# A Strassen MLP on one core: seven left operands made one by one, or six of them in pairs

## The chip, the cores and the metric

One core of a Trainium2 chip runs the whole program. A NeuronCore has TensorE (PE: matmuls, with its weight loads listed as PEld), VectorE (DVE), ScalarE (ACT), GpSimd (POOL) and SyncE (SP), which here issues the transfers. Each engine takes the instructions of its own queue in order, and one that needs a result of another engine waits at the head of its queue. The metric is the device time of one launch in microseconds; three launches were timed, and the median counts.

## What is computed

The reference is one step of a two-layer trunk for 1152 tokens (128 context, 1024 latent) of width 1024. Each layer has a mixer, and then the MLP with which this change has to do:

```python
D_MODEL = 1024
DEPTH = 2
D_FF = 4 * D_MODEL
EPS = 1e-6

def rms_norm(x, g):
    xf = x.astype(F32)
    y = xf * lax.rsqrt(jnp.mean(xf * xf, axis=-1, keepdims=True) + EPS)
    return (y * g.astype(F32)).astype(x.dtype)
...
    h2 = rms_norm(x, p['norm2']) * (1 + sc2) + sh2
    x = x + g2 * (jnp.square(jax.nn.relu(h2 @ p['w1'])) @ p['w2'])
```

`sh2`, `sc2` and `g2` come from the conditioning vector. A final RMS norm follows the last layer. Everything is float32. The kernel gets near that by splitting each operand of a product into a high part in the matmul's format and a low part, which is the remainder, and by adding three products of parts: high·high, high·low and low·high.

## The kernel before

**Seven products instead of eight.** Both products of the MLP are tiled in blocks of two by two, and each block product is formed with seven products of sums of blocks (the Strassen-Winograd form). For one block of `w2` (a *version* of the left operands, four quarters `a11`, `a12`, `a22`, `a21` of 128x256 each), the seven left operands are, in the order of the products 0 to 6: `a11`, `s1 = a22 + a21`, `s2 = s1 - a11`, `a12`, `s3 = a11 - a21`, `s4 = a12 - s2`, `a22`. The right operands come from `hidden_operands`: `B11`, `T1`, `T2`, `B21`, `T3`, `B22`, `T4`, made of the MLP's hidden values, which are read back from `hd` in tiles `xb`.

**The left operands.** `Weights.version` is a generator. For each of the seven it takes one tile `wt` of 128x512, writes the high part with a ScalarE cast (`acopy`, L184) and the low part as a difference (`psub` on POOL, L187, or `vsub` on DVE, L190):

```python
def part(t):
    o = new().rearrange("p (j c) -> p j c", j=2)
    acopy(o[:, 0], t)
    next(subs)(o[:, 1], t, o[:, 0])
    return o
```

`lo_subs(n)` hands n of the seven differences to DVE: four (operands 1, 3, 5, 6) in the first three versions of a layer, two (3, 6) in all others. The raw quarters lie in two tiles `wr` (`a11|a12` and `a22|a21`), the sums `s1` to `s4` in two tiles `wl`, made by four DVE additions of 128x256 per version. The ring `W2_RING` has 11 tiles: `release(i)`, called behind the last use of operand i, makes the operand 10 places after the oldest one not yet released.

**The lines.** `second(g, m, q)` with `Line.products` runs the seven products of one block product. A product is two blocks deep, with three matmuls in each (L1103 high·high, L1104 high·low, L1105 low·high), so 6 matmuls, and 42 in a line:

```python
a = pb("bA")[:, :BLK]
run(a, 0, True)
acopy(bb, a)
...
run(bb, 2)
acopy(bc, bb)
```

Product 0 lies in PSUM tile `bA`; ScalarE copies it to `bB`, product 2 is added there, ScalarE copies that to `bC`; products 3, 4, 5 and 6 are then added to `bA`, `bB`, `bC` and once more `bB`. Product 1 has a tile `bE` of its own. As each sum is complete, an operation `row<-bA`, `row<-bB` or `row<-bC` (DVE in all but the first group: L196, in the last group L208) adds it to the result rows. `Line.add` weaves the first four products of one line between the last ones of the line before; there are two `bB` and two `bC`, used in turn, so product 2 of a line has to wait until the line before the last has left its `bB`.

**Order.** A layer has 64 lines, in 8 groups of the hidden width, and 36 versions (five in the first group, four in each of the six middle ones, seven in the last, where most versions serve one line). The program is written in the order of the calls; a scheduler, which weighs priorities (`tc.high_priority`) and its own estimate of the durations, writes each engine's queue from it. In the last group the norm of the result starts (`rms_rest`), behind which come the next layer's operands or the output `y`.

Of the kernel before, what the change touches and what calls it, by code (L numbers as in the profile page):

```python
# [6 lines left out]
F32 = mybir.dt.float32  # L7
# [36 lines left out]
HALF, BLK, GRID, CTXH = T // 2, T // 4, TS // 2, TP // 2  # L44
W1_RING, W2_RING = (7, 7), 11
MID = (28, 28, 30, 31, 32, 33, 34, 35, 36, 37)
HEAD, FOOT, TAIL = 4, 2, 300
LOADS = 5, 2
URGE1, URGE2 = 400, 400
MLP_MODS = (6, 32)  # L50
W1_SUBS, W2_SUBS = (2, 8, 2, 5), (4, 3, 2)
HIDDEN_SUBS = (0, 0, 1, 0, 0, 1, 1)
# [68 lines left out]
def build(ctx, tc, I, O):  # L121
# [39 lines left out]
    def phase(st, tag, bufs, w=NW, side="left"):  # L161

        pool = st.enter_context(tc.tile_pool(name=tag, bufs=bufs, side=side, reuse_waits="tile"))
        return lambda name, dt=F32: pool.tile([P, w], dt, tag=tag, name=name)
# [48 lines left out]
    def dma(out, in_):  # L213
        return nc.sync.dma_start(out=out, in_=in_)
# [131 lines left out]
    def rms_rest(sq, ps=None, w=P):  # L346
        return rms_turn(rms_scale(sq, ps or pb, w), ps or pb, w)
# [661 lines left out]
    class Ends:  # L1009


        def __init__(self, p5, c11, c12, c21, c22):
            self.p5, self.c11, self.c12, self.c21, self.c22 = p5, c11, c12, c21, c22

    def lo_subs(n):

        return iter([vsub if (i + 1) * n // 7 > i * n // 7 else psub for i in range(7)])

    class Weights:
# [51 lines left out]
        def release(self, i):  # L1071
            self.free.add(i)
            while self.low in self.free:
                self.low += 1
            self.get(min(self.low + self.ring, self.total) - 1)

    class Line:
# [236 lines left out]
    for l in range(DEPTH):  # L1314
# [418 lines left out]
        tp = [two_phases(st0, "tp0", 6, 1, T)]  # L1733
        ring2 = phase(st0, "wt", W2_RING, 4 * P, "right")
        z_ = phase(st0, "z5", 4, BLK, "right")
        tp += [two_phases(st1, "tp1", 5, 2, T), phase(st1, "tp2", 7, T, "right")]

        def group_operands(s):
# [9 lines left out]
            [(m, (0,)) for m in range(KD // 2 - 1)] + [(KD // 2 - 1, (0, 1))] + [(m, (1,)) for m in reversed(range(KD // 2 - 1))]]  # L1748
        weights = Weights([I["w2"][l, g, m] for g in range(NG) for m, _ in order[g]], 2, lambda: ring2("wt", F32R), W2_RING,
                          lambda i: lo_subs(W2_SUBS[0] if i < W2_SUBS[1] else W2_SUBS[2]))  # L1750
        line = Line(banks, weights)

# [69 lines left out]
        for k in range(2):  # L1822
            sums[done[1]].add(rows[2 * done[0] + k])
        rs = [rms_rest(t, pa, (b - a) // 3) for t, (a, b) in zip(sums[1].sq, cut[n0:])]
        if last:
# [131 lines left out]
```

## Time and profile before

| | before |
|---|---|
| three timed runs | 3304.11, 3305.46, 3312.4 us; median 3305.46 |
| profiled execution | 3315.0 us (span 3313.2 us, mean granted clock 0.952) |
| busy, share of the span | PE 90%, PEld 85%, DVE 73%, ACT 50%, POOL 44% |
| second product of the MLP, layer 0 | about 1256 to 1699 us of the span |
| second product of the MLP, layer 1 | about 2841 to 3290 us of the span |

The profiled execution is one of its own, 9.5 us above the median of the three others. A span counts from the first to the last instruction. The shares are means over the whole program; the second product is 443 us of each layer, and what goes on there is read from its own windows. Matmuls overlap in the records, so a busy share near 100% is no proof of the full rate; the number of matmuls in a window says more.

### The profile page before, as it was taken

Reading aid. Unit: us, or ns where it says so; the run is one execution under the profiler, and the core shown is the slowest. Engines: PE = TensorE matmul, PEld = TensorE weight load, DVE = VectorE, ACT = ScalarE, POOL = GpSimd, SP = SyncE. Lnnn points to the kernel's source line nnn. Section 1 sums busy time; section 2 is a strip of 40 time slices with the busy share of each in tenths; the row PEclk is TensorE's granted clock in tenths of the full one; section 3 lists DMA queues with packets and bytes.
Section 4 is the critical chain, followed back from the end, with each engine's and each line's share of the span. In section 5 each row is a group of like instructions: output and inputs, shape, how many; then the busy total and the mean of one; then the engine's idle time right before and its main releaser. Section 6 shows DMA issues by size and latency. Waiting matters only on the chain. (4 is left out here: it accounts for less than half of the span.)

```text
span 3313.2 us, 60910 instructions
## 1 busy us (share of the span) xinstructions
PE 2981.6 (90%) x21208; PEld 2819.6 (85%) x21208; DVE 2415.0 (73%) x5467; ACT 1662.5 (50%) x4089; POOL 1468.4 (44%) x1400
## 2 busy tenths in 40 slices
PE   7888998998888898999868999999989999899985
PEld 6877888798888897899868889988879999789985
DVE  7899973677899967888983677345777223788897
ACT  5543244564644456455454533455637556654443
POOL 4442132444533335666535321334555343565663
PEclk8999999999999998999979999999999999999997
DMA  7342448983455553322422112689534333323242
GB/s 265 92 108 94 131 124 237 279 265 106 137 181 173 171 158 100 96 88 88 128 98 75 58 37 72 192 252 293 184 129 133 106 98 112 111 90 98 93 128 67
DMA packets 363220, 451.11 MB, mean 136 GB/s; under 512 B 64416, under 2 KB 238624, under 8 KB 362912
## 3 DMA queue, kind: packets, MB, share of 16 engines
q1 hardware_dynamic: 362912, 447.22, 44.4%
q8 instruction: 167, 2.74, 0.3%
q14 instruction: 141, 1.16, 0.1%
HBM read 338.29 MB, written 108.79 MB: 135 GB/s over the span
## 5 line engine op out<-in xcount | busy, mean ns | idle before, releaser
L187 POOL TENSOR_TENSOR wl<-wr,wh 128x512 fp32r<-128x512 f32 x164 | 229.4, 1402 | 482.2 <-ACT wh L184 367.8
L187 POOL TENSOR_TENSOR ws<-wl,ws 128x512 fp32r<-128x512 f32 x160 | 222.9, 1397 | 334.9 <-ACT ws L184 327.4
L1103 PE MATMUL bB<-T,wt 128*128 128x288 f32 x768 | 243.0, 318 | 81.5 <-ACT bB L184 46.3
L187 POOL TENSOR_TENSOR wt<-wl,wt 128x256 fp32r<-128x256 f32 x276 | 256.6, 938 | 106.4 <-ACT wt L184 77.0
L1103 PE MATMUL bB<-t,ws 128*128 128x288 f32 x768 | 235.1, 307 | 48.3 <-DVE hr L196 34.8
L211 ACT ACTIVATE hr<-hr 128x288 f32<-128x288 f32 x384 | 170.2, 445 | 200.9 <-DVE hr L196 194.3
L414 PE MATMUL pj<-hh,wh 128*128 128x384 f32 x640 | 223.7, 354 | 24.5 <-ACT g L211 11.4
L280 DVE CUSTOM_DVE_ANT_0 junk<-wm,sil,ma 128x384 bf16<-128x384 f32 (+1 forms) x320 | 233.1, 728 | 10.1 <-DMA wm<-in_w_mod 4.2
L1103 PEld LDWEIGHTS bB<-T,wt 128*128 128x128 f32 x768 | 149.5, 195 | 103.0 <-ACT bB L184 58.0
L1104 PE MATMUL bB<-T,wt 128*128 128x288 f32 x768 | 232.9, 304 | 0.0
L1105 PE MATMUL bB<-T,wt 128*128 128x288 f32 x768 | 231.7, 303 | 0.0
L1105 PE MATMUL bB<-t,ws 128*128 128x288 f32 x768 | 230.0, 300 | 0.0
L1104 PE MATMUL bB<-t,ws 128*128 128x288 f32 x768 | 229.9, 299 | 0.0
L416 PE MATMUL pj<-hh,wl 128*128 128x384 f32 x640 | 225.5, 353 | 4.6 <-POOL wl L187 4.6
L415 PE MATMUL pj<-hh,wh 128*128 128x384 f32 x640 | 224.2, 351 | 0.0
L1103 PEld LDWEIGHTS bB<-t,ws 128*128 128x128 f32 x768 | 147.9, 193 | 60.0 <-DVE hr L196 40.6
L190 DVE TENSOR_TENSOR xb<-xb 128x576 f32<-128x576 f32 (+1 forms) x160 | 169.5, 1061 | 10.0 <-POOL B L187 6.9
L414 PE MATMUL wo<-u,wh 128*128 128x288 f32 x512 | 161.3, 316 | 16.7 <-DVE x L208 13.4
L184 ACT CAST wh<-wr 128x512 fp32r<-128x512 f32 x164 | 101.6, 621 | 129.9 <-PE pj L415 72.4
L1103 PE MATMUL bA<-B,wt 128*128 128x288 f32 x512 | 158.1, 311 | 8.6 <-DVE row L208 3.0
L184 ACT CAST wt<-wl 128x256 fp32r<-128x256 f32 x288 | 115.9, 407 | 91.4 <-PE bB L1105 42.3
L1105 PE MATMUL bA<-B,wt 128*128 128x288 f32 x512 | 156.4, 306 | 3.8 <-POOL wt L187 3.8
(345 smaller groups left out, 11143.0 us busy)
## 6 DMA issues: line engine op xcount, KB each, us to landing
wr<-in_w SPq DMA_DIRECT2D x304, 256.0 KB, 3.0
xb<-hd SPq DMA_DIRECT2D x64, 576.0 KB, 4.0
wm<-in_w_mod SPq DMA_DIRECT2D x160, 192.0 KB, 2.9
wr<-in_w_in SPq DMA_DIRECT2D x104, 256.0 KB, 2.9
bi<-in_bias SPq DMA_DIRECT2D x96, 192.0 KB, 4.4
QS<-qd SPq DMA_DIRECT2D x72, 256.0 KB, 4.3
hd<-hr SPq DMA_DIRECT2D x128, 144.0 KB, 2.8
hd<-hr SPq DMA_DIRECT2D x128, 112.0 KB, 2.1
```

What stands on the lines that cost most here:

```text
L184: nc.scalar.copy(out=out, in_=in_)
L187: nc.gpsimd.tensor_tensor(out=out, in0=a, in1=b, op=ALU.subtract)
L190: nc.vector.tensor_tensor(out=out, in0=a, in1=b, op=ALU.subtract)
L211: nc.scalar.activation(out=out, in_=in_, func=f, **kw)
L280: nc.vector.tensor_tensor_reduce(out=junk[:, :w], in0=r[:, :w], in1=sil[:, c, k0:k0 + w], scale=1.0, scalar=acc[c], op0=ALU.mult, op1=ALU. ...
L414: mm(ps, lhsT=wh(k), rhs=ah(k), start=k == first, stop=False)
L415: mm(ps, lhsT=wh(k), rhs=al(k), start=False, stop=False)
L416: mm(ps, lhsT=wl(k), rhs=ah(k), start=False, stop=k == last)
L1103: mm(ps, lhsT=w[:, 0, ti(i)], rhs=t[:, 0], start=start and i == 0, stop=False, skip_group_check=True)
L1104: mm(ps, lhsT=w[:, 0, ti(i)], rhs=t[:, 1], start=False, stop=False, skip_group_check=True)
L1105: mm(ps, lhsT=w[:, 1, ti(i)], rhs=t[:, 0], start=False, stop=i == n - 1, skip_group_check=True)
```

## The change

Six of the seven left operands are made in three pairs: `a11` with `a12` (products 0 and 3), `s1` with `s3` (1 and 4), `s2` with `s4` (2 and 5). The raw tile `a11|a12` is a pair as it is loaded; the sums are laid into two tiles so that the other pairs stand side by side. One cast and one difference of 128x512 make both high parts and both low parts of a pair; `a22` (product 6) stays alone. The ring of 11 tiles of 128x512 becomes five tiles of 128x1024 (`wt`) and one of 128x512 (`wu`, for `a22`), the same number of bytes. A pair's tile is free when both products have been released, and `wu` when product 6 of the version before has been. The differences' engines are now given for the three pairs and the single: DVE, POOL, DVE, POOL in the first three versions, POOL, POOL, DVE, POOL in the others. The last `rms_rest` is put at a higher priority.

```diff
-W1_RING, W2_RING = (7, 7), 11
+W1_RING, W2_RING = (7, 7), (5, 1)
-URGE1, URGE2 = 400, 400
+URGE1, URGE2, URGE3 = 400, 400, 60
-W1_SUBS, W2_SUBS = (2, 8, 2, 5), (4, 3, 2)
+W1_SUBS = (2, 8, 2, 5)
...
+    def w2_subs(i):
+
+        return (vsub, psub, vsub, psub) if i < 3 else (psub, psub, vsub, psub)
+
...
+    class PairWeights(Weights):
...
+            def part(t, o):
+                acopy(o[:, 0], t)
+                next(subs)(o[:, 1], t, o[:, 0])
+                return o
+
+            def pair(t):
+                o = part(t, new().rearrange("p (j c) -> p j c", j=2))
+                later.append(o[:, :, w:])
+                return o[:, :, :w]
+
+            yield pair(raw[0])
+            s, r = (W.tile([P, DM // 2], F32, tag="wl", name="wl") for _ in range(2))
+            s1, s3, s2, s4 = s[:, :w], s[:, w:], r[:, :w], r[:, w:]
+            vtt(s1, a22, a21, ALU.add)
+            vsub(s3, a11, a21)
+            yield pair(s)
+            vsub(s2, s1, a11)
+            vsub(s4, a12, s2)
+            yield pair(r)
+            yield from later
+            yield part(a22, self.new1().rearrange("p (j c) -> p j c", j=2))
+
+        def ready(self, i):
+
+            v, p = divmod(i, 7)
+            if p == 6:
+                j = v - self.ring[1]
+                return j < 0 or 7 * j + 6 in self.free
+            j, k = divmod(3 * v + p - self.ring[0], 3)
+            return p > 2 or j < 0 or {7 * j + k, 7 * j + k + 3} <= self.free
+
+        def release(self, i):
+            self.free.add(i)
+            while len(self.tiles) < self.total and self.ready(len(self.tiles)):
+                self.get(len(self.tiles))
...
-        ring2 = phase(st0, "wt", W2_RING, 4 * P, "right")
+        ring2, ring1 = phase(st0, "wt", W2_RING[0], 8 * P, "right"), phase(st0, "wu", W2_RING[1], 4 * P, "right")
...
-        weights = Weights([I["w2"][l, g, m] for g in range(NG) for m, _ in order[g]], 2, lambda: ring2("wt", F32R), W2_RING,
-                          lambda i: lo_subs(W2_SUBS[0] if i < W2_SUBS[1] else W2_SUBS[2]))
+        weights = PairWeights([I["w2"][l, g, m] for g in range(NG) for m, _ in order[g]], 2, lambda: ring2("wt", F32R),
+                              lambda: ring1("wu", F32R), W2_RING, lambda i: iter(w2_subs(i)))
...
-        rs = [rms_rest(t, pa, (b - a) // 3) for t, (a, b) in zip(sums[1].sq, cut[n0:])]
+        with tc.high_priority(URGE3):
+            rs = [rms_rest(t, pa, (b - a) // 3) for t, (a, b) in zip(sums[1].sq, cut[n0:])]
```

In the changed kernel the three matmuls stand at L1161, L1162 and L1163. The queues of the two kernels differ within the two second products only; the numbers behind the names count tiles and differ from kernel to kernel.

ScalarE's queue, middle groups of layer 0. Before, the casts of one version are the seven rows `wt` (`wr_18162` is its `a11|a12`, `wr_18164` its `a22|a21`, the `wl` its sums), with the copies of the lines between them:

```order
L184 CAST wt_18166<-wr_18162 128x256
L184 CAST wt_18215<-wl_18213 128x256
L184 CAST wt_18234<-wl_18213 128x256
L184 CAST wt_18251<-wr_18162 128x256
L184 CAST wt_18271<-wl_18269 128x256
L184 COPY bB_10171<-bA_18199 128x288
L184 CAST wt_18290<-wl_18269 128x256
L184 COPY bB_10172<-bA_18262 128x288
L184 CAST B11_18469<-xb_18465 128x576
L184 CAST wt_18307<-wr_18164 128x256
```

ScalarE's queue at a like place in the changed kernel:

```order
L184 CAST wt_17855<-wl_17789 128x512
L184 COPY bB_10171<-bA_17859 128x288
L184 CAST wt_17909<-wr_17905 128x512
L184 CAST T4_18009<-xb_17985 128x576
L184 CAST wt_17916<-wl_17912 128x512
L184 COPY bC_10173<-bB_10171 128x288
L184 CAST wu_17902<-wr_17783 128x256
L184 COPY bB_10172<-bA_17927 128x288
```

Three wide casts and one narrow one now stand for the seven, and the `a22` of a version (`wu_17902`) stands behind the first two pairs of the next one.

POOL's queue at such a place, before (`T3`, `B11`, `T1` and `B21` are low parts of right operands):

```order
L187 TENSOR_TENSOR wt_17920<-wl_17918,wt_17920 128x256
L187 TENSOR_TENSOR T3_17895<-xb_17875,T3_17895 128x576
L187 TENSOR_TENSOR wt_17939<-wl_17918,wt_17939 128x256
L187 TENSOR_TENSOR wt_17976<-wl_17974,wt_17976 128x256
L187 TENSOR_TENSOR B11_18174<-xb_18170,B11_18174 128x576
L187 TENSOR_TENSOR wt_17995<-wl_17974,wt_17995 128x256
L187 TENSOR_TENSOR T1_18178<-xb_18170,T1_18178 128x576
L187 TENSOR_TENSOR wt_18033<-wr_18029,wt_18033 128x256
```

and in the changed kernel:

```order
L187 TENSOR_TENSOR wt_17785<-wr_17781,wt_17785 128x512
L187 TENSOR_TENSOR wt_17792<-wl_17788,wt_17792 128x512
L187 TENSOR_TENSOR wu_17778<-wr_17630,wu_17778 128x256
L187 TENSOR_TENSOR T1_17991<-xb_17983,T1_17991 128x576
L187 TENSOR_TENSOR B21_17999<-xb_17985,B21_17999 128x576
L187 TENSOR_TENSOR T3_18003<-xb_17983,T3_18003 128x576
L187 TENSOR_TENSOR wt_17909<-wr_17905,wt_17909 128x512
L187 TENSOR_TENSOR wt_17916<-wl_17912,wt_17916 128x512
```

A version's low parts on POOL now stand together, and up to three right operands' parts of 128x576 stand between one version's and the next one's.

TensorE's queue in the middle groups of layer 0, around a product 2, before:

```order
L1103 MATMUL bB_10171<-T2_17593,wt_17939 128x288
L1104 MATMUL bB_10171<-T2_17593,wt_17939 128x288
L1105 MATMUL bB_10171<-T2_17593,wt_17939 128x288
L1103 MATMUL bB_10171<-T2_17593,wt_17939 128x288
L1104 MATMUL bB_10171<-T2_17593,wt_17939 128x288
L1105 MATMUL bB_10171<-T2_17593,wt_17939 128x288
```

and in the changed kernel, where `wt_17855` is a pair `s2|s4` and `wt_17785` the pair `a11|a12`:

```order
L1161 MATMUL bB_10171<-T2_17442,wt_17855 128x288
L1162 MATMUL bB_10171<-T2_17442,wt_17855 128x288
L1161 MATMUL bA_17859<-B21_17445,wt_17785 128x288
L1162 MATMUL bA_17859<-B21_17445,wt_17785 128x288
L1163 MATMUL bA_17859<-B21_17445,wt_17785 128x288
L1161 MATMUL bA_17859<-B21_17445,wt_17785 128x288
L1162 MATMUL bA_17859<-B21_17445,wt_17785 128x288
L1163 MATMUL bA_17859<-B21_17445,wt_17785 128x288
L1163 MATMUL bB_10171<-T2_17442,wt_17855 128x288
L1161 MATMUL bB_10171<-T2_17442,wt_17855 128x288
```

Product 2 begins with the two matmuls that need only the high part of `s2`, product 3 stands in between, and the first matmul with the low part (L1163) follows it.

## Rows read from the trace of the kernel before

**Rows 1.** The page's first line and its busy times by engine.
```profile
span 3313.2 us, 60910 instructions
...
PE 2981.6 (90%) x21208; PEld 2819.6 (85%) x21208; DVE 2415.0 (73%) x5467; ACT 1662.5 (50%) x4089; POOL 1468.4 (44%) x1400
```

**Rows 2.** Busy time by window; columns as the first line says.
```profile
core 0: us, PE busy (x) PEld busy (x) DVE busy (x) ACT busy (x) POOL busy (x), PEclk, DMA share, GB/s
1256.00:1350.00 94.00, 77.93 (x474) 73.77 (x475) 79.15 (x102) 59.51 (x154) 63.20 (x54) 0.83 0.31 97
1350.00:1600.00 250.00, 236.30 (x1711) 229.66 (x1711) 212.89 (x397) 124.00 (x293) 151.99 (x142) 0.99 0.31 95
1600.00:1699.00 99.00, 78.32 (x519) 74.23 (x517) 93.97 (x192) 48.19 (x117) 48.21 (x46) 0.89 0.41 128
2740.00:2800.00 60.00, 60.00 (x455) 60.00 (x454) 18.22 (x29) 36.25 (x81) 19.75 (x16) 1.00 0.33 104
2835.00:2950.00 115.00, 95.49 (x625) 90.90 (x625) 91.76 (x127) 69.39 (x178) 70.33 (x62) 0.90 0.32 100
2950.00:3200.00 250.00, 235.07 (x1706) 227.74 (x1705) 216.63 (x400) 123.79 (x293) 152.39 (x142) 1.00 0.33 100
3200.00:3290.00 90.00, 66.55 (x422) 63.16 (x420) 82.08 (x174) 42.98 (x111) 43.67 (x43) 0.84 0.25 77
```

**Rows 3.** TensorE's waits from 1350 to 1600 us: total us, times, longest.
```profile
PE bB L1103 <- ACT bB L184: 9.2, 12, 1.1
PE bB L1103 <- ACT bC L184: 3.4, 4, 0.9
PE bB L1103 <- DVE row L196: 0.7, 3, 0.3
PE bA L1103 <- DVE row L196: 0.3, 1, 0.3
```

**Rows 4.** TensorE's waits from 2950 to 3200 us.
```profile
PE bB L1103 <- ACT bB L184: 9.5, 14, 1.1
PE bB L1103 <- ACT bC L184: 3.9, 5, 0.9
```

**Rows 5.** Timeline of DVE: start, us, instruction, [idle before <- releaser].
```profile
1437.01 1.66 DVE L190 TENSOR_TENSOR wl<-wl,wr 128x256 f32<-128x256 f32 x1
...
1443.05 0.96 DVE L190 TENSOR_TENSOR B<-xb,B 128x576 fp32r<-128x576 f32 x1 [0.23 <-ACT B L184]
1443.93 0.45 DVE L196 TENSOR_TENSOR row<-bB,row 128x288 f32<-128x288 f32 x1
```

**Rows 6.** Timeline of ACT, the same place.
```profile
1444.41 0.38 ACT L184 COPY bB<-bA 128x288 f32<-128x288 f32 x1 [0.47 <-DVE row L196]
```

**Rows 7.** Timeline of PE, the same place.
```profile
1444.85 0.40 PE L1103 MATMUL bB<-T,wt 128*128 128x288 f32 x1 [0.89 <-ACT bB L184]
```

**Rows 8.** Groups by line and shape: busy us, mean ns, idle before and releasers.
```profile
L187 POOL TENSOR_TENSOR wt<-wl,wt 128x256 fp32r<-128x256 f32 x276 | 256.6, 938 | 106.4 <-ACT wt L184 77.0 <-DVE row L196 17.4 <-issue 8.0
L187 POOL TENSOR_TENSOR ws<-wl,ws 128x512 fp32r<-128x512 f32 x160 | 222.9, 1397 | 334.9 <-ACT ws L184 327.4 <-DVE mod L280 4.9 <-DMA hd<-hr 1.9
L184 ACT CAST wt<-wl 128x256 fp32r<-128x256 f32 x288 | 115.9, 407 | 91.4 <-PE bB L1105 42.3 <-PE bA L1105 23.1 <-DVE wl L190 13.8
L184 ACT CAST ws<-wl 128x512 fp32r<-128x512 f32 x160 | 98.3, 618 | 64.4 <-PE bB L1105 23.3 <-PE bC L1105 14.6 <-PE bA L1105 11.9
L190 DVE TENSOR_TENSOR wt<-wr,wt 128x256 fp32r<-128x256 f32 x144 | 94.9, 659 | 19.7 <-ACT wt L184 19.2
L184 ACT CAST wt<-wr 128x256 fp32r<-128x256 f32 x216 | 87.4, 407 | 27.9 <-PE bC L1105 13.2 <-PE bB L1105 6.4 <-PE bA L1105 5.3
L187 POOL TENSOR_TENSOR wt<-wr,wt 128x256 fp32r<-128x256 f32 x72 | 65.1, 904 | 81.1 <-PE bA L1105 38.6 <-ACT wt L184 25.4 <-DVE wl L190 15.5
L190 DVE TENSOR_TENSOR ws<-wr,ws 128x512 fp32r<-128x512 f32 x52 | 41.7, 802 | 18.2 <-ACT ws L184 18.1
```

**Rows 9.** DVE's differences of line 190: duration ns min/median/max, first and last start.
```profile
L190 DVE TENSOR_TENSOR wt<-wr,wt x144: 406/426/1628, 1257.5 to 3262.0; 128x256 fp32r<-128x256 f32 x144
...
L190 DVE TENSOR_TENSOR ws<-wr,ws x52: 676/688/1780, 826.5 to 2829.9; 128x512 fp32r<-128x512 f32 x52
```

**Rows 10.** Timeline of PE at the end of either layer: first matmul of the last product.
```profile
1694.84 0.61 PE L1103 MATMUL bB<-T,wt 128*128 128x288 f32 x1 [9.78 <-DVE row L208]
...
3283.77 0.61 PE L1103 MATMUL bB<-T,wt 128*128 128x288 f32 x1 [7.35 <-DVE row L208]
```

**Rows 11.** Timeline of POOL around the first row of Rows 5.
```profile
1436.50 1.89 POOL L187 TENSOR_TENSOR T<-xb,T 128x576 fp32r<-128x576 f32 x1 [1.40 <-ACT T L184]
```

**Rows 12.** POOL's differences of line 187, 1350 to 1600 us: ns min/median/max.
```profile
L187 POOL TENSOR_TENSOR T<-xb,T x20: 1425/1870/1953, 1366.5 to 1589.6; 128x576 fp32r<-128x576 f32 x20
```

More of the change, by code (lines that the diff above doesn't have):

```diff
@@ L1075, in release, with __init__, version @@
             self.get(min(self.low + self.ring, self.total) - 1)
+    class PairWeights(Weights):
+        def __init__(self, srcs, n, new, new1, rings, subs):
+            self.new1 = new1
+            super().__init__(srcs, n, new, rings, subs)
+        def version(self, src, n, new, subs, spare):
+            w = n * P
+            raw = []
+            for i in range(2):
+                t = W.tile([P, DM // 2], F32, tag="wh" if i else "wr", name="wr")
+                dma(t, src[:, 2 * i * w:2 * (i + 1) * w])
+                raw.append(t)
+            a11, a12 = (raw[0][:, j * w:(j + 1) * w] for j in range(2))
+            a22, a21 = (raw[1][:, j * w:(j + 1) * w] for j in range(2))
+            later = []
+            def part(t, o):
[28 more added lines that the diff above has]
+                self.get(len(self.tiles))
     class Line:
```

## The prediction, made before the changed kernel ran

> **What bounds the kernel now.** I read the page first. TensorE is busy for 90% of the span and ScalarE and POOL, which the change relieves most, for half of it or less [rows 1], so the number to find is not how much work goes away but how much of TensorE's lost time hangs on it. For that the windows over the two second products count matmuls. [...]
>
> Then who is waited for. In the middle, TensorE names almost one thing: product 2 waits for the copy from `bA` to `bB`, 9.2 us in 12 waits and 9.5 in 14; the copy from `bB` to `bC` costs 3.4 in 4 and 3.9 in 5 [rows 3, 4]. [...] No left operand is waited for. The timeline of one such wait gives the chain: DVE's difference for a right operand runs 0.96 us, behind it DVE reads the old `bB` into the rows (0.45), then ScalarE copies (0.38), then the matmul starts after 0.89 us idle [rows 5, 6, 7]. So the wait is the bank's, and the late one is DVE, which is 85% and 87% busy there; in the two last stretches it is busy for 94 of 99 and 82 of 90 us [rows 2], and there it is the bound.
>
> **The change part by part.** Prices first; a 512-wide difference or cast exists already in the first product (`ws`), the same shape and format, so I take its mean.
> DVE: of the 72 versions, 6 (three a layer) lose four differences of 0.659 and get two of 0.802, 1.03 us less each; the other 66 lose two and get one, 0.52 less each [rows 8]. That is 40 us of DVE in all. The wide difference could cost from 0.676, the least seen of its shape, to 1.32, twice the narrow one's mean [rows 8, 9], so 0.52 lies between 0.64 and nothing.
> ScalarE: 504 casts of 0.407 (203 us) become 216 of 0.618 and 72 of 0.407 (163), 40 us less. POOL: 256.6 + 65.1 us become 138 differences of 1.397 and 72 of 0.904 (258), 64 less [rows 8]. Neither is a bound (ScalarE 50%, POOL 61% busy in the middle [rows 2]), so I count these at nothing by themselves; DVE's and TensorE's waits cover them.
> The rest of the instructions, transfers among them, keep their number: raw tiles are loaded as before, and the four sums stay four. The higher priority of the last norm I cost at nothing: without it every queue of the changed kernel comes out in the same order.
>
> What moves is the order. I counted matmuls in TensorE's two queues. From the end of product 6 on a `bB` to the next product 2 on it there were 22 in the mean and now are 26: 4 x 0.132 = 0.53 us more room for the chain above. From the end of product 2 to product 4 on the same bank, which needs the copy to `bC` in between, there were 18 and now are 13: 0.66 us less. And a weight tile's old contents used to be done with 100 matmuls (13 us, median) before the new low part was wanted; in the middle groups it is now 37 (4.9 us), at least 27 (3.6 us), and for a high part 25 (3.3 us), at least 19 (2.5).
>
> A, the middle (1711 and 1706 matmuls of 84 a version make 41 versions [rows 2]): the 26 waits for `bB` average 18.7 / 26 = 0.72 us, so 0.53 more room removes most of each but not all: 26 x 0.53 = 13.8, of which I take 12, since the longest go to 1.1. The 9 waits for `bC` would grow by 0.66 each if each stayed where it is: 9 x 0.66 = 6 lost. What then remains, 6.7 for `bB` and 13.3 for `bC`, 20 us, is still behind DVE's queue, and DVE does 41 x 0.52 = 21 us less. A wait is shortened only where the saved piece stood in front of a read of its bank; no row gives that share, so it lies between 0 and 20, and I take 8, somewhat under half. Sum: -12 + 6 - 8 = -14, with bounds of +6 (no gain on `bB`) and -26 (all 26.0 us of waits gone).
> B, the last groups: DVE is the bound, so its saving counts whole: 7 versions x 0.52 = 3.6 a layer, -7. Against it `wu` is a ring of one tile: the very last `a22` can be cast only when the product 6 before is over, and its chain of 0.407 and 0.904 [rows 8] stands 1 to 3 matmuls ahead of its use. But the last product waits 9.78 and 7.35 us for DVE's rows anyway [rows 10]; I count +1 a layer. Sum: -5.
> C, the starts: three versions x 1.03 = 3.1 a layer on DVE, which is 80 to 84% busy; half of it counts: -3.
> Together -22. The profiled execution took 3315.0 us, of which 3313.2 are the span [rows 1]; it would be 3293. It lies 9.5 over the median of the three runs, which I carry over: 3293 - 9.5 = 3283.5.
>
> [...] First the row: a DVE sum of 128x256 at 1437.01 took 1.66 us [rows 5], where DVE's difference of the same size has a median of 0.426 and a maximum of 1.628 [rows 9]; POOL's difference of 128x576 ran from 1436.50 to 1438.39 [rows 11], and DVE's instruction ended just after it. [...]
>
> **The rivals.**
> Slower: the ring is too short. A pair's tile needs both of its products done, then a cast (0.618), then a difference on POOL (1.397) [rows 8]: 2.0 us with empty queues, against 3.6 to 4.9 us to the low part's use. One right operand's difference in front on POOL (median 1.87 [rows 12]) makes it 3.9, two make it 5.8. POOL is 61% busy, and up to three stand there together in its new queue; the queue's order fits this (matmuls with the low part are put later, behind product 3), if the scheduler's durations are right. Against it: nothing of `wt` is waited for in the middle now [rows 3, 4]. A mean new wait of 22 / 72 = 0.31 us a version eats the gain; at 1.0 us, about half of what one more POOL difference in front would bring, the 72 versions cost 72, less the 22: 3315 + 50 - 9.5 = 3355; at 0.7 us, 50 - 22 = +28, 3333. I put this rival at 3333.
> [...]
> No change: the middle's waits only move from `bB` to `bC`, since DVE is as late as before, and the ends alone gain: B and C, -8, 3297.
> More: the waits of the middle vanish (-26), the ends gain DVE's saving whole (-7 and -6), with no cost of `wu`: -39, 3266.
>
> **How the numbers follow.** 0.3% (10 us) is about what a measurement of this kernel can tell from no change. The forecast, 3275 to 3294, has 0.46: the prices are those of the same shapes, and DVE is the engine late in each of the three stretches. More has 0.14; the lock 0.10 and no change 0.10; the short ring 0.20, since the room was cut by 8 us and the queues are planned to a microsecond. Faster is 0.46 + 0.14 = 0.60, the same 0.20, slower 0.20. The range goes from 3262, under "more", to 3318, which takes in a mild case of the short ring (0.5 us a version: 36 - 22 = +14, 3319) and leaves its worse half and a few in a hundred at the lower end outside. The likeliest case's own range is its bounds: 3275 to 3294.
>
> **What would show it.** Right: casts of 128x512 near 0.62 us and differences near 1.4 (POOL) and 0.8 (DVE); in the middle windows about 243 us for the matmuls that now take 250, less "bB from ACT", perhaps more "bC from ACT"; no wait of product 2 or 5 for ScalarE's or POOL's `wt`. Wrong: TensorE waiting at L1161 for ScalarE's cast of `wt` or `wu`, or at L1163 for POOL's or DVE's difference, tens of times; a DVE that is busier than before in spite of fewer instructions; or the ends of the stages, which DVE bounds, no shorter.

## The result, and the profile after

The changed kernel took 3329.68 us in the median of four runs (3323.36 to 3330.45), the kernel before 3306.69 of four: ratio 1.0061, 95% interval [1.0048, 1.0075]. It is slower by 0.6%, 23 us, where 0.7% faster was forecast. The two profiled executions show 8.4 of these 23 (3323.4 against 3315.0), since the one after is the lowest of its four and the one before lies above its median. Counted from the first matmul with a left operand of `w2` to the last, the two second products together took 888.6 us before and take 903.9 now, 15.3 more; the rest of the program, whose queues are the same in both, was 7 us shorter in the execution after. So the profiles account for the direction, the places, and some two thirds of the size. The granted clock is not behind it: 0.952 in the execution before, 0.959 in the one after, and 0.99 to 1.00 in the middles of both.

The windows of the changed kernel, against [rows 2] (the first, second and fifth are the same stretches):

```profile
core 0: us, PE busy (x) PEld busy (x) DVE busy (x) ACT busy (x) POOL busy (x), PEclk, DMA share, GB/s
1256.00:1350.00 94.00, 80.15 (x536) 73.68 (x536) 75.77 (x97) 55.69 (x127) 57.74 (x40) 0.95 0.34 107
1350.00:1600.00 250.00, 228.05 (x1662) 221.68 (x1661) 230.81 (x374) 113.15 (x229) 141.30 (x99) 1.00 0.29 93
1600.00:1702.00 102.00, 78.23 (x500) 73.30 (x498) 96.47 (x180) 44.59 (x94) 44.73 (x33) 0.90 0.36 117
2838.00:2950.00 112.00, 96.58 (x630) 89.42 (x629) 89.22 (x115) 66.26 (x149) 65.66 (x46) 0.92 0.31 97
2950.00:3200.00 250.00, 227.08 (x1654) 220.48 (x1652) 230.35 (x370) 110.12 (x223) 140.54 (x98) 1.00 0.31 96
3200.00:3299.00 99.00, 71.66 (x453) 66.91 (x452) 88.65 (x177) 44.09 (x99) 41.30 (x34) 0.84 0.26 81
```

The start of layer 0 gained: 62 matmuls more in the same 94 us, 8 us of work at 0.132 each (455 in 60.00 us at a granted clock of 1.00 [rows 2]). But the stage began 3 us earlier there (1253.1 for 1256.2), and the granted clock was 0.95 for 0.83, so not all of this is the change's. The middles lost: 49 and 52 matmuls fewer in 250 us each, 13 us together; and DVE, which has fewer instructions there (374 for 397, 370 for 400), is busy for 231 and 230 us where it was for 213 and 217. Fewer instructions, and 92% busy: this is the row to stop at. DVE's groups in the whole changed kernel say which instructions (count, busy us, mean ns, idle before and what ended it). The four sums `s1` to `s4` are the groups that write `wl` of 128x256:

```profile
L190 DVE TENSOR_TENSOR wl<-wr 128x256 f32<-128x256 f32 x72 | 69.8, 970 | 0.0
L190 DVE TENSOR_TENSOR wt<-wl,wt 128x512 fp32r<-128x512 f32 x72 | 64.8, 899 | 1.9 <-ACT wt L184 1.7
L190 DVE TENSOR_TENSOR wl<-wr,wl 128x256 f32<-128x256 f32 x72 | 59.1, 821 | 0.7
L190 DVE TENSOR_TENSOR wl<-wl,wr 128x256 f32<-128x256 f32 x72 | 57.5, 798 | 13.9 <-POOL wt L187 12.8 <-POOL ws L187 0.6
L196 DVE TENSOR_TENSOR wl<-wr 128x256 f32<-128x256 f32 x72 | 49.5, 688 | 7.7 <-POOL ws L187 5.0 <-DMA wr<-in_w 2.4
L190 DVE TENSOR_TENSOR wt<-wr,wt 128x512 fp32r<-128x512 f32 x6 | 8.1, 1349 | 5.2 <-ACT wt L184 5.2
...
L196 DVE TENSOR_TENSOR row<-bB,row 128x288 f32<-128x288 f32 x192 | 85.0, 447 | 14.5 <-PE bB L1163 14.4
```

and the same four sums in the kernel before, with the same reading of a bank:

```profile
L190 DVE TENSOR_TENSOR wl<-wl,wr 128x256 f32<-128x256 f32 x72 | 53.8, 748 | 0.3
L190 DVE TENSOR_TENSOR wl<-wr 128x256 f32<-128x256 f32 x72 | 47.7, 662 | 5.9 <-POOL wt L187 5.3 <-POOL ws L187 0.6
L190 DVE TENSOR_TENSOR wl<-wr,wl 128x256 f32<-128x256 f32 x72 | 38.5, 534 | 0.1
L196 DVE TENSOR_TENSOR wl<-wr 128x256 f32<-128x256 f32 x72 | 35.1, 488 | 5.1 <-POOL ws L187 5.0
...
L196 DVE TENSOR_TENSOR row<-bB,row 128x288 f32<-128x288 f32 x192 | 86.1, 449 | 39.7 <-PE bB L1105 39.3
```

The four sums of a version, 288 instructions of one shape in both kernels, took 175.1 us before and take 235.9 now. The reading of a bank, whose first operand lies in PSUM, takes the same 0.45. The timeline shows what a slow sum stands beside. DVE in the middle of layer 0 (start, us):

```profile
1458.43 1.51 DVE L196 TENSOR_TENSOR wl<-wr 128x256 f32<-128x256 f32 x1
1459.86 0.45 DVE L196 TENSOR_TENSOR row<-bB,row 128x288 f32<-128x288 f32 x1
1460.23 1.15 DVE L190 TENSOR_TENSOR wl<-wr 128x256 f32<-128x256 f32 x1
1461.30 0.45 DVE L196 TENSOR_TENSOR row<-bC,row 128x288 f32<-128x288 f32 x1
```

POOL at the same time:

```profile
1458.16 1.49 POOL L187 TENSOR_TENSOR wt<-wr,wt 128x512 fp32r<-128x512 f32 x1 [1.25 <-ACT wt L184]
1459.62 1.49 POOL L187 TENSOR_TENSOR wt<-wl,wt 128x512 fp32r<-128x512 f32 x1
```

The first sum ends at 1459.94, POOL's first pair at 1459.65; the second sum ends at 1461.38, POOL's second pair at 1461.11: each ends 0.3 us behind POOL's instruction. The bank's reading between them runs beside POOL in its usual 0.45. All sums of the trace say the same. Of the 288, 149 begin with no POOL instruction under way (or with less than 0.1 us of it left), and none of these takes more than 0.43 us. The other 139 are met by one, and take 1.25 us in the mean. Of these, 127 take more than 0.6 us, and each of the 127 ends 0.28 or 0.29 us behind the end of a POOL instruction. In the kernel before 92 were met, at 1.02 us in the mean, and 74 took more than 0.6, each again ending 0.28 or 0.29 us behind POOL. So the change has more sums met, and for longer. No reading of a bank takes more than 0.52, met or not.

TensorE's waits from 1350 to 1600, against [rows 3]:

```profile
PE bB L1161 <- ACT bB L184: 8.1, 6, 1.4
PE bA L1161 <- DVE row L196: 7.0, 6, 1.5
PE bB L1161 <- ACT bC L184: 3.3, 4, 0.8
PE bB L1161 <- DVE row L196: 2.4, 2, 1.4
PE bE L1163 <- POOL wt L187: 1.0, 1, 1.0
PE bA L1163 <- POOL wt L187: 0.2, 1, 0.2
```

The copy to `bB` is waited for half as often, the copy to `bC` as before; DVE's reading of `bA` is new, 7.0 for 0.3. Left operands are waited for twice, 1.2 us in all.

The starts and ends of the stages look different. TensorE's waits for left operands from 1250 to 1705, before:

```profile
PE bA L1105 <- POOL wt L187: 1.4, 2, 1.1
PE bA L1103 <- ACT wt L184: 1.4, 1, 1.4
```

and in the changed kernel:

```profile
PE bA L1163 <- DVE wt L190: 3.1, 1, 3.1
PE bA L1161 <- ACT wt L184: 1.9, 2, 1.6
PE bE L1163 <- POOL wt L187: 1.4, 2, 1.0
PE bE L1161 <- ACT wt L184: 1.0, 1, 1.0
PE bB L1163 <- POOL wu L187: 0.7, 1, 0.7
PE bB L1163 <- DVE wt L190: 0.5, 1, 0.5
PE bA L1163 <- POOL wt L187: 0.2, 1, 0.2
```

Added up over both second products, TensorE's waits for banks (for a copy into one, or for its reading into the rows) grew from 83 to 97 us, those for left operands from 8 to 20, and those for right operands fell from 13 to 7.

### The profile page after: what moved, and what is told of

It is laid out like the page before. It is cut to its first block, busy times and chain, and to the rows that moved or that the text cites. A ratio compares the mean times of both kernels' runs of the same rounds, so it can differ in the third digit from the quotient of the medians.

```text
span 3321.4 us, 60403 instructions
## 1 busy us (share of the span) xinstructions
PE 2974.2 (90%) x21208; PEld 2803.9 (84%) x21208; DVE 2454.4 (74%) x5389; ACT 1629.8 (49%) x3873; POOL 1435.0 (43%) x1262
## 5 line engine op out<-in xcount | busy, mean ns | idle before, releaser
L1161 PE MATMUL bB<-t,ws 128*128 128x288 f32 x768 | 234.9, 307 | 48.1 <-DVE hr L196 34.9
L1162 PE MATMUL bB<-t,ws 128*128 128x288 f32 x768 | 230.1, 300 | 0.2 <-DVE t L190 0.2
L1163 PE MATMUL bB<-t,ws 128*128 128x288 f32 x768 | 229.7, 299 | 0.0
L1161 PEld LDWEIGHTS bB<-t,ws 128*128 128x128 f32 x768 | 147.4, 192 | 59.5 <-DVE hr L196 40.5
L190 DVE TENSOR_TENSOR xb<-xb 128x576 f32<-128x576 f32 (+1 forms) x160 | 175.1, 1097 | 23.2 <-POOL B L187 18.7
L1161 PE MATMUL bB<-T,wt 128*128 128x288 f32 x512 | 158.6, 310 | 32.3 <-ACT bB L184 20.6
L1161 PE MATMUL bA<-B,wt 128*128 128x288 f32 x512 | 157.4, 309 | 22.7 <-DVE row L196 18.4
L414 PE MATMUL wo<-u,wh 128*128 128x288 f32 x512 | 160.6, 315 | 16.3 <-DVE x L208 13.6
L187 POOL TENSOR_TENSOR B<-xb,B 128x576 fp32r<-128x576 f32 x64 | 93.4, 1459 | 176.7 <-ACT B L184 170.5
L1163 PE MATMUL bA<-B,wt 128*128 128x288 f32 x512 | 155.0, 304 | 7.6 <-DVE wt L190 6.4
L184 ACT CAST T<-xb 128x576 fp32r<-128x576 f32 x128 | 86.2, 673 | 144.8 <-DVE xb L190 137.8
L415 PE MATMUL wo<-u,wh 128*128 128x288 f32 x512 | 153.8, 301 | 2.8 <-DMA u<-ud 2.8
L1162 PE MATMUL bA<-B,wt 128*128 128x288 f32 x512 | 154.0, 301 | 2.2 <-POOL B L187 2.1
L1163 PE MATMUL bB<-T,wt 128*128 128x288 f32 x512 | 154.0, 301 | 1.0 <-DVE wt L190 1.0
```

Source lines behind the costliest of these rows:

```text
L184: nc.scalar.copy(out=out, in_=in_)
L187: nc.gpsimd.tensor_tensor(out=out, in0=a, in1=b, op=ALU.subtract)
L190: nc.vector.tensor_tensor(out=out, in0=a, in1=b, op=ALU.subtract)
L414: mm(ps, lhsT=wh(k), rhs=ah(k), start=k == first, stop=False)
L415: mm(ps, lhsT=wh(k), rhs=al(k), start=False, stop=False)
L1161: mm(ps, lhsT=w[:, 0, ti(i)], rhs=t[:, 0], start=start and i == 0, stop=False, skip_group_check=True)
```

## The experiments

Theory A: DVE's sums and differences of SBUF operands stand still while POOL's instruction runs, and DVE is the late engine. Theory B: the pairs come late or in bursts whatever their width, so the ring and the order cost the time. Every edit makes the scheduler write all queues anew, so no run changes one thing alone. In the table, "ratio" is to the kernel before, with its interval, and "sums" is the time of the four sums, added from their four groups (at 0.41, the least of one, it would be 118). "Met" is how many of the 288 sums are met by a POOL instruction, and their mean time. "Waits" are TensorE's in both second products, for banks and for left operands. The last four columns are from the one profiled execution of each run. The medians are from several sessions; the ratios compare across them.

| run | median us | ratio | sums us | met | DVE busy | waits |
|---|---|---|---|---|---|---|
| before | | 1 | 175.1 | 92, 1.02 | 2415.0 | 83, 8 |
| changed | 3329.68 | 1.0061 [1.0048, 1.0075] | 235.9 | 139, 1.25 | 2454.4 | 97, 20 |
| e1 POOL in halves | 3318.03 | 1.0036 [1.0022, 1.0049] | 222.1 | 167, 1.02 | 2425.5 | 92, 21 |
| e2 all narrow | 3314.63 | 1.0019 [1.0010, 1.0028] | 209.2 | 147, 1.02 | 2430.3 | 83, 27 |
| e3 DVE, POOL, DVE, POOL | 3307.99 | 1.0004 [0.9995, 1.0013] | 203.2 | 117, 1.13 | 2447.7 | 79, 25 |
| e4 all on POOL | 3341.83 | 1.0096 [1.0082, 1.0111] | 249.9 | 162, 1.22 | 2447.1 | 97, 23 |
| e5 other pair on DVE | 3317.36 | 1.0020 [1.0010, 1.0030] | 205.7 | 119, 1.14 | 2421.8 | 74, 35 |
| e6 e3 with halves | 3299.42 | 0.9966 [0.9953, 0.9979] | 184.3 | 104, 1.04 | 2422.1 | 73, 18 |
| e7 four short buffers | 3338.63 | 1.0085 [1.0072, 1.0098] | 238.6 | 138, 1.28 | 2456.6 | 100, 20 |
| e8 e7, two `wu` | 3348.06 | 1.0108 [1.0089, 1.0126] | 231.7 | 141, 1.21 | 2435.8 | 100, 14 |
| e9 fills | 3265.65 | 0.9870 [0.9851, 0.9889] | 157.8 | 161, 0.65 | 2324.1 | 56, 15 |
| e10 before, halves | 3318.33 | 1.0026 [1.0016, 1.0035] | 179.3 | 129, 0.88 | 2410.3 | 94, 8 |
| e11 before, four on DVE | 3303.21 | 0.9981 [0.9971, 0.9992] | 145.1 | 57, 0.87 | 2433.2 | 79, 7 |
| e12 e6, `hidden` halves | 3289.69 | 0.9931 [0.9917, 0.9946] | 166.2 | 108, 0.85 | 2395.9 | 47, 39 |
| e13 copies | 3322.87 | 1.0033 [1.0020, 1.0047] | 167.0 | 122, 0.80 | 2358.4 | 81, 18 |
| e14 e3, all narrow | 3313.73 | 1.0014 [1.0004, 1.0025] | 160.1 | 64, 1.06 | 2429.8 | 74, 31 |
| e15 e11 with halves | 3317.72 | 1.0026 [1.0017, 1.0035] | 161.1 | 87, 0.90 | 2425.4 | 91, 7 |

**e1, POOL's pairs in halves.**

```diff
-                next(subs)(o[:, 1], t, o[:, 0])
+                sub = next(subs)
+                for c in range(0, t.shape[-1] if sub is psub else w, w):
+                    e = c + w if sub is psub else t.shape[-1]
+                    sub(o[:, 1, c:e], t[:, c:e], o[:, 0, c:e])
```

> The changed kernel, with each 128x512 difference on POOL written as two of 128x256; casts, DVE's differences, tiles and rings stay. Theory A (DVE's sums and differences of SBUF operands stand still while a wide POOL instruction runs, and DVE is the late engine): in the middle of layer 0 the time of DVE's instructions over the least of their shape falls from 59 us towards 45, and the kernel gets back some 15 to 25 of the 23 us, 3305 to 3315. Theory B (pairs come late or in bursts whatever their width, so the ring and the order cost the time): no change against the changed kernel, 3325 to 3335, with POOL's total up by some 60 us.

3318.03: between the two ranges, nearer to A's; 8 us come back by the ratios (0.25% of 3307), with POOL 27 us busier in all. The sums give back 14 us: a met sum costs what it did before, 1.02, but 167 are met. That speaks against B. It is no clean proof of A, since in the profiled executions the two second products are as long as in the changed kernel (903.0 for 903.9), and what this execution saved lies outside them.

**e2, everything narrow.** As e1, with the cast in the loop too, and DVE's pair as well.

> The changed kernel with its pair tiles and its rings, but both the casts and the differences of a pair written as two of 128x256 (ScalarE and DVE too): only the pairing and the ring of the change remain, none of its wide instructions. Theory A: about the time of the kernel before, 3300 to 3312. Theory B: the loss stays, 3322 to 3340.

3314.63, outside both ranges, 6 us over the kernel before (0.19%): with the wide instructions gone some two thirds of the loss are gone, and a third stays with pairing. The waits show which third: those for banks are back at the 83 of the kernel before, those for left operands are 27 for 8.

**e3, DVE, POOL, DVE, POOL.**

```diff
-        return (vsub, psub, vsub, psub) if i < 3 else (psub, psub, vsub, psub)
+        return (vsub, psub, vsub, psub)
```

> The changed kernel with the engines of the first three versions in all: the differences of the first and the third pair on DVE, of the second on POOL. DVE gets 66 more wide differences of 0.68 us at least (45 us), POOL 66 fewer of 1.4. Theory A: what DVE stands still falls by about half (from 170 us in both second products to 90 or 100), which pays for the 45: 3310 to 3330, no slower than the changed kernel. Theory B: DVE is the late engine and has 45 us more to do: 3345 to 3370.

3307.99, the time of the kernel before, 22 us under the changed one (0.57% by the ratios), although DVE makes 66 wide differences more. POOL's instructions for left operands fall from 287.7 to 175.0 us, and the sums give back 33 us. This is the plainest run against B, and better than A expected: the sums, 203, are still above 175, and DVE's total fell by 7 only.

**e4, all on POOL.** The line of e3 with `(psub, psub, psub, psub)` from the fourth version on.

> The changed kernel with all three pairs' differences on POOL from the fourth version on: DVE has 66 differences of 0.83 us less (55 us), POOL 66 of 1.4 more. Theory A: DVE stands still longer by about half as much again per version, some 50 us, which eats the saving: 3320 to 3340, the same as the changed kernel. Theory B: less work on the late engine DVE pays, unless weights are waited for: 3295 to 3315 with few waits for POOL's differences, or over 3340 with tens of them.

3341.83, 2 us over A's range: the engine that is late got 55 us less to do by the expectation, its total fell by 7, and the kernel is 12 us slower. B's second range (over 3340) asks for tens of waits for POOL's differences; there are 17 in both layers, 10 us, where the changed kernel has 9, 7 us. That is 3 us more, against 14 us more in the sums.

**e5, the second pair on DVE.** The line of e3 with `(psub, vsub, psub, psub)` from the fourth version on.

> The changed kernel with DVE making the difference of the second pair in place of the third from the fourth version on: as many and as wide instructions on each engine as in the changed kernel, in another phase. Theory A, in the form that counts only how much wide work POOL has: no change, 3325 to 3335. Theory A, in the form that it matters which of POOL's differences run beside DVE's sums (now the first pair's beside the sums s1 and s3, the second pair's beside s2 and s4): the second of these meetings goes, and 8 to 15 us come back, 3313 to 3322. Theory B: no change.

3317.36: with the same number and widths of instructions on every engine, the sums take 30 us less and the kernel 12. Which of POOL's instructions run beside the sums matters, as much as how wide they are. This is A's second form; A's first form, which counts only how much wide work POOL has, and B both failed. Some of what the banks gave back (74 for 97) went to left operands (35 for 20).

**e6, e3 with POOL's pair in halves**, the edits of e1 and e3 together.

> The experiment with DVE, POOL, DVE, POOL in all versions, and POOL's one wide difference per version written as two of 128x256. Theory A: splitting gave 11 us where two wide ones a version were split, so it gives about half here, 3300 to 3306, and would beat the kernel before by a few us. Theory B: no change from 3308.

3299.42, 0.34% under the kernel before, as A said: this version beats both kernels.

**e7 and e8, the ring.** For a second `wu` a buffer of another pool was given up; e7 is the control.

```diff
-    F = ctx.enter_context(tc.tile_pool(name="short", bufs=5))
+    F = ctx.enter_context(tc.tile_pool(name="short", bufs=4))
...
-W1_RING, W2_RING = (7, 7), (5, 1)
+W1_RING, W2_RING = (7, 7), (5, 2)
```

> The changed kernel with four in place of five short buffers in the pool that gives room to the next experiment: its control. The queues in the middle of the second product stay as they are. Both theories: as the changed kernel, 3324 to 3336, if the fewer buffers cost nothing elsewhere.

> The control with a second buffer for the single operand a22 (five pair tiles and two singles). Theory B (the short ring is the cause): the cast of a22 no longer waits for the product 6 before it, which holds up the copies queued behind it on ScalarE: 6 to 12 us less than the control. Theory A: within 4 us of the control.

The control is 3338.63, somewhat slower than expected; the second `wu` gave 3348.06, slower still, outside both ranges. It took 6 us off the waits for left operands (14 for 20), so the single buffer of `a22` has a part in them, but the time did not follow. Nor did it follow DVE, which was 21 us less busy than in the control; what made this run slow was not found. A longer ring of pairs was not tried.

**e9, fills in place of differences.**

```diff
-                next(subs)(o[:, 1], t, o[:, 0])
+                sub = next(subs)
+                if sub is psub and t.shape[-1] > w:
+                    for c in range(3):
+                        nc.gpsimd.memset(o[:, 1].bitcast(F32), 0.0)
+                else:
+                    sub(o[:, 1], t, o[:, 0])
```

> The changed kernel, in which POOL writes a constant (three fills of 128x512) where it made a pair's difference, so that these instructions read nothing; those low parts are left out of the result, and no longer wait for the cast. Theory A (DVE's sums stand still because POOL reads SBUF operands beside them): DVE's time over the least of each shape falls in the middle of layer 0 from 54.6 us to under 35, although POOL runs 150 instructions more, and the time to 3295 to 3312. Rival (DVE is slowed by any work of POOL, or by something that has nothing to do with POOL): it stays above 45 us.

3265.65, 64 us under the changed kernel and below A's range. "Over the least" is worked out from DVE's instructions in layer 0 from the 17th line's copy to `bB` to the 49th's: each one's time less the least of its group there, added up. It is 54.5 us in the changed kernel, 34.4 before, 21.6 here. (The expectations have the first as 59 in e1, and the last as 25 in e13; the figures in the text are all counted in one way.) POOL's fills, and one of the sums:

```profile
L1104 POOL MEMSET wt<- 128x512 f32 x414 | 205.0, 525 | 130.2 <-PE bB L1168 124.2 <-PE bA L1168 0.7
...
L190 DVE TENSOR_TENSOR wl<-wr 128x256 f32<-128x256 f32 x72 | 42.2, 586 | 0.0
```

POOL spends 205 us on them, about the 212 of the pairs' differences, and the same sum takes 0.59 for 0.97. But the pairs' low parts are left out and a fill waits for no cast, so the time is not one that a whole kernel could have. What DVE does beside a fill is a cleaner result. Two sums in a row, and four fills at the same time:

```profile
1411.85 0.41 DVE L190 TENSOR_TENSOR wl<-wl,wr 128x256 f32<-128x256 f32 x1
1412.30 0.42 DVE L190 TENSOR_TENSOR wl<-wr,wl 128x256 f32<-128x256 f32 x1
...
1410.83 2.04 POOL L1104 MEMSET wt<- 128x512 f32 x4
```

Of the 161 sums that are met, 108 are met by a fill, and none of these takes more than 0.43; the 53 met by a difference take 1.13 in the mean. The fills, which read nothing, hold no sum.

**e13, copies in their place**: `nc.gpsimd.tensor_copy(out=o[:, 1], in_=t)` twice, where e9 has three fills.

> As the experiment with the fills, but POOL copies the operand (two copies of 128x512) where it wrote a constant: these instructions read SBUF, and wait for the cast as little as the fills did; the low parts of these pairs are wrong by what is left out. Theory A: DVE stands still beside them again, 40 us or more over the least of each shape in the middle of layer 0 against 25 with the fills, and the time is 15 to 40 us above 3266. Rival (what made the fills fast is that low parts came early): the time stays within 8 us of 3266 and DVE's excess near 25.

Both forecasts of the time failed: it is above either range. Over the least it is 21.0 us, where A said 40 and the rival near 25. The copies read SBUF, but they are short:

```profile
L1104 POOL CAST wt<-wl 128x512 fp32r<-128x512 f32 x144 | 109.9, 764 | 38.8 <-PE bB L1168 20.9 <-PE bC L1168 15.0 <-issue 1.5
...
L190 DVE TENSOR_TENSOR wl<-wr 128x256 f32<-128x256 f32 x72 | 44.2, 614 | 0.0
```

The copies take 0.76 and 0.78 us, where the differences took 1.59 and 1.49 in the changed kernel, so a sum that is met has less to stand still for. But stand still it does. One sum, and the copy that meets it:

```profile
1453.98 0.83 DVE L196 TENSOR_TENSOR wl<-wr 128x256 f32<-128x256 f32 x1
...
1453.39 1.14 POOL L1104 CAST wt<-wr 128x512 fp32r<-128x512 f32 x1
```

The sum ends 0.28 us behind the copy. Of 122 sums met, 87 are met by a copy, and take 0.65 in the mean and up to 0.84, where the 108 beside a fill kept to 0.43. So in the two runs together reading is what matters: beside the differences (1.13 us in the mean in e9) and the copies (0.65), which read SBUF, a sum is held, and beside the fills (0.43 at most), which only write, it is not.

The time of the whole is another matter. Counted by TensorE's matmuls, the middle 32 lines of both layers take 391 us with the copies, as long as in the kernel before (391) and 13 us shorter than in the changed kernel (404). The last 16 lines take 278 us, where the changed kernel takes 265. The 57 us between the two runs are in the first 16 lines (239 us with the copies, 212 with the fills) and in the last 16 (278 and 238), not in the middle (391 and 393). Why the ends are long with the copies was not found.

**e10, the kernel before with halves**, in `hidden_operands`:

```diff
-            (vsub if next(subs) else psub)(o[:, 1], t, o[:, 0])
+            if next(subs):
+                vsub(o[:, 1], t, o[:, 0])
+            else:
+                for i in range(2):
+                    psub(o[:, 1, i], t[:, i], o[:, 0, i])
```

> The kernel before, with POOL's 128x576 differences for right operands written as two of 128x288 each: the same lever on the kernel before, where the change has no part. Theory A: DVE's lengthened instructions (sums of xb above all) stand still for less, 5 to 8 us less in the middle of a layer, and the time falls by 5 to 10 us. Rival (the length of POOL's instructions does not matter, the pairs' phase alone did it): no change, or some us slower, since POOL is busier by 20 to 40 us.

3318.33, slower by 0.26%: A missed, and the rival, that it would be no faster or some us slower, came true. The sums stay at 179: a met sum costs less (0.88 for 1.02), but 129 are met for 92, and POOL is 40 us busier. Shorter instructions alone are no gain here.

**e11, the kernel before with four of seven differences on DVE**: `W2_SUBS = (4, 3, 4)`.

> The kernel before, with four of seven differences on DVE in all versions, as it has in the first three: the share of the engines in the experiment with DVE, POOL, DVE, POOL, without pairs. DVE gets 132 differences of 0.41 us at least more (54 us), POOL 132 fewer. Theory A: what DVE stands still falls by 30 to 40 us, which does not quite pay: 3308 to 3320. Rival (the experiment with DVE, POOL, DVE, POOL was fast because POOL was relieved, whatever the width): 3295 to 3303.

3303.21, at the edge of the rival's range and 5 us under A's: relieving POOL pays without any pair, 0.19%, with the sums down to 145.

**e12, e6 with the halves of e10.**

> The fastest experiment so far (DVE, POOL, DVE, POOL, with POOL's wide difference in two), and POOL's 128x576 differences in two as well. Theory A: again 5 to 10 us less, 3290 to 3296. Rival: no change from 3299, or slower, since POOL has 20 to 40 us more to do.

3289.69, 0.69% under the kernel before, the fastest that computes everything, at the edge of what A said, although POOL is 39 us busier than in e6.

**e14 and e15, with and without pairs.** e14 has the edits of e2 and e3, e15 those of e10 and e11.

> Pair tiles and rings of the change, every cast and difference in two of 128x256, and DVE, POOL, DVE, POOL in all versions: four of seven differences on DVE, two halves and the single on POOL. Against the kernel before with four of seven on DVE (ratio 0.998) only the pairing is left. Theory A alone (the pairing itself costs nothing, width and phase do): 3296 to 3304. Rival (the pairing costs some 6 us, as the first experiment with narrow instructions showed): 3306 to 3313.

> The kernel before without pairs, with four of seven differences on DVE and POOL's 128x576 differences in halves, to stand beside the fastest experiment (3290). If the pairs have a gain of their own once POOL does little beside DVE's sums: 3298 to 3308, slower than 3290. If the gain came from the share of the engines and the halves: 3285 to 3293.

e14 against e11 has the same share of the engines and the same widths, and pairs: 1.0014 against 0.9981, so pairing itself costs about 0.33%, 11 us; 3313.73 is just over the rival's range, and 10 us over that of A alone. The sums take 15 us more, but DVE is as busy and the waits for banks are fewer (74 for 79). What is new are the waits for left operands, 31 us for 7, and one at the head of DVE's queue. The sum `s1` in e14, and in e11:

```profile
L196 DVE TENSOR_TENSOR wl<-wr 128x256 f32<-128x256 f32 x72 | 36.9, 512 | 21.0 <-DMA wr<-in_w 15.5 <-POOL ws L187 5.3
```

```profile
L196 DVE TENSOR_TENSOR wl<-wr 128x256 f32<-128x256 f32 x72 | 34.3, 476 | 5.3 <-POOL ws L187 5.0
```

It waits 15.5 us for raw tiles. Such waits stand in every kernel with pairs (2.4 us in the changed one, 22.2 in e2) but e8, where a second `wu` lets `a22` be cast earlier, and in none without pairs; so a raw tile is probably kept until its `a22` is cast. e15 against e12 went the other way: 3317.72 is outside both of its ranges, and with the halves, the pairs are 28 us faster. So pairs are worth something in one arrangement and cost in another; why halves hurt both unpaired kernels stays open.

## Why the prediction was wrong

**The step that failed is DVE's.** "That is 40 us of DVE in all" less; DVE became busier by 39 (2454.4 against 2415.0). The term had two parts. The differences came out near their price: 105.9 us before (94.9 [rows 8] and 11.0 for the six versions' others) are 72.9 now, 33 less for 40, at 0.899 for the 0.802 taken. The other part had no price: "the four sums stay four" put them at nothing, and they took 60.8 us more. The rest of DVE's instructions took 12 more, of which the differences of `T` took 11. The prediction itself had named "a DVE that is busier than before in spite of fewer instructions" as a sign of being wrong. An operation that a change does not touch can still change its duration by what runs beside it: the sums took 0.61 us each before and take 0.82 now.

To set stretches of the same work side by side, the next three parts go by TensorE's matmuls: 2688 a layer, of which 672 are the first 16 lines' worth, 1344 the middle 32 lines' and 672 the last 16 lines'. The 0.132 us a matmul in the forecast is 60.00 us by 455 at a granted clock of 1.00 [rows 2].

**A, the middle: -14 forecast.** The two middles took 403.5 us for 391.2, +12. The room for the chain to `bB` was right: fewer waits for it. But DVE's time over the least of each group (as worked out in e9) went from 34.4 to 54.5 us in layer 0 and from 34.9 to 54.5 in layer 1, 39.7 in all. Its busy time grew by 31.6, since its own work fell by 8. Its idle time took up 19.7 of that, and the other 11.9 are what the stretch grew by. TensorE waited there 32 us for banks (22 before) and 3 for left operands (none before).

**B, the last groups: -5 forecast.** The last 16 lines took 264.9 us for 255.1, +10. "DVE is the bound, so its saving counts whole" held with the sign turned: between the copies to `bB` of the 49th and the 64th line DVE is busy for 108 of 113 us and 107 of 113, and its time over the least is 27 and 26 us, where it was 19 and 21 before.

**C, the starts: -3 forecast.** The first 16 lines took 234.6 us for 241.4, 7 less, 4.7 of them in layer 0, where the granted clock was 0.95 for 0.83. Right in sign, then, but how much of it is the clock no run separates. There, three of nine versions already have the shares of e3. Left operands, which the prediction had read as never waited for from the middles alone, cost 13 us of waits here (7 before).

**ScalarE and POOL.** ScalarE's saving came (busy 1629.8 for 1662.5, 33 of the 40) and nothing points to a worth of its own, as said. POOL's pair differences took 1.59 and 1.49 for the 1.40 taken, and `a22`'s 1.05 for 0.90, so it saved 34 for 64.

**The rivals.** The short ring, to which 0.20 was given, has the time (3333 against 3329.7) and a part of the mechanism. Left operands are waited for 20 times in both second products, 20 us together (8 times and 8 us before). But that is 12 us more, where the rival took 50, and only 3 of the 20 us are in the middles. The lock, at 0.10, by which a longer POOL instruction holds a DVE instruction beside it for longer, has the mechanism of the larger part (a met sum takes 1.25 us for 1.02 before). Its price was far too low: 16 us, the author's estimate, a quarter of the 63 us of 138 differences longer by 0.46 us [rows 8], where the sums alone took 60.8 us more. It counted only the longer instruction, not that the first pair's and the second pair's differences now run just when DVE makes the sums (in e5, with the second pair's on DVE, 119 are met for 139). That POOL was to have 64 us less to do was the wrong comfort: 139 sums are met for 92. What counts is when.

Named rightly, the loss has two parts. The larger is DVE standing still: it shows in the sums, and in TensorE's waits for banks, 15 us more in the changed kernel. These waits are back at 83 or less where the sums are relieved (e2, e3, e5, e6, e14). The smaller comes with pairing, and shows in TensorE's waits for left operands, 12 us more: they are 7 to 8 us in all four kernels without pairs and 14 to 39 in all with them, and they stay when the sums are relieved (27 in e2, where the kernel is 0.19% behind; 31 in e14, 0.33% behind e11). The waits do not simply add up to the time: e12 has the most for left operands and is the fastest of all that compute everything. What keeps the pairs late, the ring's length or the queues' order, is not settled, nor is what the halves cost in the kernels without pairs, where the waits for banks grow (94 for 83 in e10, 91 for 79 in e15).

The higher priority of the last norm moved no instruction: without it the changed kernel's queues are the same, and with it alone so are those of the kernel before.

The runs agree with each other on DVE's standing still: of the sums that are met, each over 0.6 us ends 0.28 or 0.29 us behind a POOL instruction in the kernel before and in the changed one, a bank's reading keeps its 0.45, and sums are held by differences (1.25 us in the mean in the changed kernel) and copies (0.65 in e13), not by fills (0.43 at most in e9).

## What to carry to other kernels

When a change makes POOL's instructions longer or moves them, price the DVE instructions of two SBUF operands that will run beside them, the untouched ones first: how many of them will begin while POOL reads SBUF, and how long each will be held. Here a sum met by POOL's instruction took 1.25 us in the mean, one not met 0.43 at most, and the 288 sums went from 0.61 to 0.82 us, since both numbers grew. Before a saving on the late engine is counted, ask what the engine will stand beside when it is due; an assignment that gave DVE 45 us more to do (e3) was 22 us faster than one that gave it less. Wide instructions are worth trying on DVE and ScalarE (DVE's differences and ScalarE's work took 33 us less each here), with POOL's kept short and few (e6), and the arrangement has to be timed as a whole, since what one engine gains another can lose (e10 and e15 against e12).

## What the runs showed that was not expected

The same splitting of POOL's 128x576 differences made the kernel 10 us faster on top of e6 (3289.69 for 3299.42) and 9 us slower on the kernel before (3318.33 for 3309.65). POOL is slower too: a 128x512 difference of a pair took 1.59 us in the changed kernel, where the first product's takes 1.40 [rows 8]; what slows it was not tried.
